# The S5 loop of a four-branch decoder layer in another order, with its outputs put in order by transfers

## The chip, the cores and the metric

The kernel runs on one core of a Trainium2 chip. The metric is the device time of one execution, in microseconds (us); less is better. A core has five engines that work side by side and wait for one another by semaphores: TensorE (PE in the profile; its weight loads are PEld), VectorE (DVE), ScalarE (ACT), GpSimd (POOL) and SyncE (SP), which here issues all transfers. Each engine takes its instructions strictly in the order of the program.

## The reference, cut to what matters

A layer runs four branches on one projected input and merges them. The change lies in branch B, a diagonal complex state-space model (S5) of 64 channel groups of 16 channels, each with one complex state of 64 dimensions:

```python
def _s5(u, state0_re, state0_im, a_re, a_im, log_dt, b_re, b_im, c_re, c_im, d_skip):
    ...
    lam_bar = jnp.exp(lam * dt)
    b_bar = ((lam_bar - 1.0) / lam)[..., None] * lax.complex(b_re.astype(f32), b_im.astype(f32))
    ug = u.reshape(bsz, t, S5_GROUPS, S5_GROUP)
    bu = jnp.einsum('gnc,btgc->btgn', b_bar, ug.astype(jnp.complex64))
    h0 = lax.complex(state0_re.astype(f32), state0_im.astype(f32))
    bu = bu.at[:, 0].add(lam_bar * h0)
    ...
    h = jax.vmap(lambda bseq: lax.associative_scan(combine, (a_el, bseq))[1])(bu)
    y = jnp.einsum('gcn,btgn->btgc', c, h).real.reshape(bsz, t, BR_WIDTH) + d_skip * u
    return y, h[:, -1].real, h[:, -1].imag
...
    y_b = jax.nn.gelu(y_b)
    y_b = y_b * jax.nn.sigmoid(jnp.matmul(y_b, s5_glu_w.astype(f32)) + s5_glu_b) * jax.nn.silu(z_s5)
```

Branch D, an attention into 256 memory tokens whose values `cache_mem_v` are read for eight samples, is touched in one place.

## The kernel before, in words

The 512 prompt tokens and the 32 tokens of eight samples lie side by side as 544 columns; the 1024 channels lie in eight tiles of 128 partitions. A large product is made in *units*: `unit` (L166) loads a tile of 1024 x 128 weights (`raw`, three buffers), ScalarE casts its high part to `whi` (L177), VectorE takes the rest to `wlo` (L64, called from L178), and TensorE makes 48 matmuls `pu` of 272 columns (L188). `whi`, `wlo` and `pu` have two buffers each.

The S5 stage runs over eight tiles f of eight groups. The prompt is cut into 64 blocks of 8 steps. `s5_in` (L708) projects `u`, reorders it on ScalarE and VectorE into `uf`, and brings it by two transfers (`ud`, `U`) to rows of step and channel. `s5_mats` (L725) builds the block matrices: powers of the transition times B (`bm`), transposed by TensorE (`pbt`) and copied to `bt`; powers times C (`cm`), where each difference of `q1` and `q2` is written by four operations of 64 partitions, since real and imaginary parts go to the lower and upper half; and from `cm` and `bbs` the Toeplitz blocks (`pk`, `kt`), spread by transfers through `kd` into `tp`. `s5_scan` (L784) makes the block inputs (`pvr`, `pvi`), turns and scans them on VectorE and GpSimd (`gr`, `gi`, `t1` to `t4`), writes the states to the halves of `hs`, their last column to `hp`, and the samples' states to `hn`, which read `pvr` and `pvi` last. `s5_y` (L838) makes `py` from `U`, `tp`, `cm` and `hs`, copies it to `yj` and takes it through DRAM (`yd`) to `yt`, with one transfer each way. There the partitions stand in the order channel, group; `s5_out` (L856) multiplies by the permutation `permid` on TensorE, which orders them as group, channel and the columns as time (`pn`), and applies GELU by ScalarE and VectorE into `stag`. `s5_rot` (L650) makes the turning factors of two tiles on GpSimd, some 36 small operations.

Between these pieces stand units of the generator `gd` (L697: gates and down projection of branch D), so that TensorE has work while the others run. The loop (L874 to L887) is, for each f: `s5_scan(f)`, `s5_mats(f+1)`, `s5_out(f-1)`, a unit, `s5_y(f)`, `s5_in(f+2)`, in most turns a second unit, and behind f = 0, 2, 4 `s5_rot`. Behind the loop come the GLU and the scan of branch A. A scheduler may move instructions past one another; what each engine runs in the end is shown below for the places that matter. Accumulators of a bank each (`bk`) come from a ring of four, shared by `pbt`, `pk`, `pvr`, `pvi`, `py` and `pn`; `bm`, `q1`, `q2`, `hs`, `yj` and `uf` have one buffer (`yj` and `uf` share one), `U` has two.

Of the kernel before, what the change touches and what calls it, by code (L numbers as in the profile page):

```python
# [34 lines left out]
def hybrid_kernel(ctx: ExitStack, tc: tile.TileContext, I, O):  # L35
# [9 lines left out]
    def ctile(shape, name, dt=F32):  # L45
        return cst.tile(shape, dt, name=name, tag=name)
# [56 lines left out]
    permid = ctile([P, P], "permid")  # L103
    V.tensor_copy(permid.rearrange("p (g c) -> p g c", c=16), ident.rearrange("p (c g) -> p g c", g=8))
# [560 lines left out]
    for b in range(NB):  # L665
        step(hd)
        step(su, 2)
        pm = xv.tile([P, 8, TS], F32, name="pmx", tag="qmx")
        tt(G, pm, pts.rearrange("p m (h t) -> p (m h) t", h=4), bc(bmask[:, b, :], 1, 8), MUL)
        for m in range(2):  # L670
            vb = xv.tile([P, D], F32, name="vb", tag="vb")
            dma(vb, I["cache_mem_v"][0, b, m * P:(m + 1) * P].rearrange("p h d -> p (h d)"))
            for h in range(4):
                T.matmul(pacc[32 * h:32 * h + 32, 0:256], pm[:, 4 * m + h, :], vb[:, h * 256:(h + 1) * 256],
                         start=b == 0 and m == 0, stop=b == 7 and m == 1, tile_position=(0, 32 * h))
# [32 lines left out]
    def s5_in(f):  # L708
        pu = unit(wcols(C_U + f * P), x2, perm=True)
        uf = s5r.tile([P, 8, NV], F32, name="uf", tag="uf", bufs=1)  # L710
        G.memset(uf[:, 4:8, 0:8], 0.0)
        G.memset(uf[:, 0:4, 72:80], 0.0)
        S.copy(uf[:, :, 8:42], pu[:, 0, 0:272].rearrange("p (k s) -> p s k", s=8))
        S.copy(uf[:, :, 42:72], pu[:, 1, 0:240].rearrange("p (k s) -> p s k", s=8))
        us = pu[:, 1, 240:272].rearrange("p (b t) -> p t b", t=4)
        V.tensor_copy(uf[:, 0:4, 0:8], us)
        V.tensor_copy(uf[:, 4:8, 72:80], us)  # L717
        U = s5r.tile([P, 8, NV], F32, name="U", tag="U", bufs=2)
        ud = s5d.tile([8, P, NV], F32, name="ud", tag="ud")
        dma(ud.rearrange("q p k -> p q k")[:, ::-1], uf)  # L720
        dma(U, ud.rearrange("q (c g) k -> (q c) g k", g=8))

        return U

    def s5_mats(f):  # L725
# [9 lines left out]
        bt = s5r.tile([P, 2, 4, P], F32, name="bt", tag="bt")  # L735
        for ri in range(2):
            pb = bank("pbt")
            for a in range(4):
                T.transpose(pb[:, a * P:(a + 1) * P], bm[:, ri, a].rearrange("p l c -> p (l c)"), ident)
            copy(S if ri else V, bt[:, ri].rearrange("p a n -> p (a n)"), pb)  # L740
# [7 lines left out]
        tt(V, q2, e4(pwi, 9), ctif, MUL)  # L748
        for g2 in range(2):
            pr = slice(64 * g2, 64 * g2 + 64)  # L750
            tt(V, cmv[0:64, :, g2], q1[pr], q2[pr], SUB)
# [3 lines left out]
        tt(G, q2, e4(pwr, 9), ctif, MUL)  # L755
        for g2 in range(2):
            pr = slice(64 * g2, 64 * g2 + 64)
            stt(cmv[64:128, :, g2], q1[pr], -1.0, q2[pr], MUL, SUB)

        bbs = s5r.tile([P, 4, 2, 16], F32, name="bbs", tag="bbs", bufs=2)  # L760
        for ri, src in enumerate((bbr, bbi)):
            for g2 in range(2):
                dma(bbs[64 * ri:64 * ri + 64, :, g2, :], src[64 * g2:64 * g2 + 64, gs])

# [19 lines left out]
    def s5_scan(f, U, bt, E):  # L784
# [35 lines left out]
        tt(G, t4, E[:, 1], gr, MUL)  # L820
        for g2 in range(2):
            pr = slice(64 * g2, 64 * g2 + 64)
            tt(V, hsv[0:64, :, g2, 9:73], t1[pr], t2[pr], SUB)
            tt(V, hsv[64:128, :, g2, 9:73], t3[pr], t4[pr], ADD)
            for ri in range(2):
                S.copy(hsv[64 * ri:64 * ri + 64, :, g2, 0:8], h0[pr, ri, :, gs].rearrange("p b a -> p a b"))
# [11 lines left out]
    def s5_y(f, U, cm, tp, hs_):  # L838
# [14 lines left out]
        dma(yt, yd.rearrange("(j c) g k -> (c g) j k", c=16))  # L853
        return yt

    def s5_out(f, yt):  # L856

        pn = [bank("pn0"), bank("pn1")]
        T.matmul(pn[0][:, 0:272], permid, yt[:, :, 8:42].rearrange("p j k -> p k j"), start=True, stop=True)
        T.matmul(pn[1][:, 0:240], permid, yt[:, :, 42:72].rearrange("p j k -> p k j"), start=True, stop=True)  # L860
        T.matmul(pn[1][:, 240:272], permid, yt[:, 0:4, 0:8].rearrange("p j b -> p b j"), start=True, stop=True)
        for a in range(2):
            y = pn[a][:, 0:HALF]
            ga = stag[f][:, a * HALF:(a + 1) * HALF]
            S.activation(ga, y, AF.Square, scale=GSQ)
            stt(ga, ga, 0.7978845608028654, y, ADD, MUL)
            S.activation(ga, ga, AF.Tanh)
            stt(ga, ga, 1.0, y, ADD, MUL)

    us_, mt_, yt = [s5_in(0)], s5_mats(0), None  # L870
# [3 lines left out]
    for f in range(8):  # L874
        bt, cm, tp, E = mt_
        hs_ = s5_scan(f, us_[f], bt, E)
        if f < 7:
            mt_ = s5_mats(f + 1)
# [3 lines left out]
        yt = s5_y(f, us_[f], cm, tp, hs_)  # L882
        if f < 6:
            us_.append(s5_in(f + 2))
        step(gd, (0, 1, 1, 1, 1, 0, 1, 1)[f])
        if f % 2 == 0 and f // 2 + 1 in range(1, 4):
            s5_rot(f // 2 + 1)  # L887
# [863 lines left out]
```

## Time and profile before

| | |
|---|---|
| median of three runs | 1483.68 us (1482.52 to 1487.28) |
| the profiled execution | 1485.23 us, of which its span is 1483.3 |
| TensorE busy | 1417.8 us, 96% of the span |
| VectorE, ScalarE, GpSimd busy | 60%, 33%, 23% |
| moved by the transfers | 172.96 MB, mean 117 GB/s |

The profile is that of one execution. A row of a group names the line, the engine, the operation, what it writes and reads, and how often; behind it come the busy time, the mean of one in ns, and how long its engine sat idle ahead of it and for whom. A row of waits says who waited for whom: sum in us, number, longest. A row of the timeline begins with start and duration; matmuls overlap, so the distance between starts is their pace.

### The profile page before, as it was taken

Reading aid. Unit: us, or ns where it says so; the run is one execution under the profiler, and the core shown is the slowest. Engines: PE = TensorE matmul, PEld = TensorE weight load, DVE = VectorE, ACT = ScalarE, POOL = GpSimd, SP = SyncE. Lnnn points to the kernel's source line nnn. Section 1 sums busy time; section 2 is a strip of 40 time slices with the busy share of each in tenths; the row PEclk is TensorE's granted clock in tenths of the full one; section 3 lists DMA queues with packets and bytes.
Section 4 is the critical chain, followed back from the end, with each engine's and each line's share of the span. In section 5 each row is a group of like instructions: output and inputs, shape, how many; then the busy total and the mean of one; then the engine's idle time right before and its main releaser. Section 6 shows DMA issues by size and latency. Waiting matters only on the chain. (4 is left out here: it accounts for less than half of the span.)

```text
span 1483.3 us, 28633 instructions
## 1 busy us (share of the span) xinstructions
PE 1417.8 (96%) x11761; PEld 1346.1 (91%) x11761; DVE 887.9 (60%) x1739; ACT 491.0 (33%) x849; POOL 338.3 (23%) x511
## 2 busy tenths in 40 slices
PE   6999998889889999999999999999999999899997
PEld 6998888778778999999999899999999998789997
DVE  5355497887877594677777544544343455454553
ACT  4244234223223432433333331333232332114232
POOL 2010233757672111002222222000000011110222
PEclk9999999999999999999999999899999999999999
DMA  8577362546536323322222464132323235663341
GB/s 204 165 214 235 105 199 65 122 95 150 121 96 131 88 80 90 86 72 78 73 77 74 115 181 135 46 89 60 93 62 89 68 111 172 200 198 115 99 147 61
DMA packets 298500, 172.96 MB, mean 117 GB/s; under 512 B 46365, under 2 KB 289385, under 8 KB 298370
## 3 DMA queue, kind: packets, MB, share of 16 engines
q1 hardware_dynamic: 298370, 171.14, 41.9%
q8 instruction: 92, 1.51, 0.4%
q14 instruction: 38, 0.31, 0.1%
HBM read 145.35 MB, written 25.24 MB: 115 GB/s over the span
## 5 line engine op out<-in xcount | busy, mean ns | idle before, releaser
L188 PE MATMUL pu<-xh,whi 128*128 128x272 f32 (+1 forms) x2000 | 430.6, 294 | 0.7 <-DVE uf L717 0.5
L188 PE MATMUL pu<-xl,whi 128*128 128x272 f32 (+1 forms) x2000 | 430.9, 293 | 0.1
L188 PE MATMUL pu<-xh,wlo 128*128 128x272 f32 (+1 forms) x2000 | 427.9, 292 | 0.0
L64 DVE TENSOR_TENSOR wlo<-raw,whi 128x1024 fp32r<-128x1024 f32 x181 | 249.4, 1378 | 220.0 <-ACT whi L177 215.9
L177 ACT CAST whi<-raw 128x1024 fp32r<-128x1024 f32 x181 | 198.6, 1097 | 485.0 <-PE pu L188 368.5
L188 PEld LDWEIGHTS pu<-xh,whi 128*128 128x128 f32 x2000 | 321.4, 191 | 6.6 <-issue 5.3
L188 PEld LDWEIGHTS pu<-xl,whi 128*128 128x128 f32 x2000 | 322.2, 191 | 5.5 <-issue 4.5
L188 PEld LDWEIGHTS pu<-xh,wlo 128*128 128x128 f32 x2000 | 319.8, 191 | 3.8 <-issue 3.3
L188 PE MATMUL pu<-oh,wlo 128*128 128x272 f32 x640 | 134.6, 290 | 2.3 <-DVE wlo L64 2.3
L188 PE MATMUL pu<-ol,whi 128*128 128x272 f32 x640 | 136.4, 291 | 0.0
L188 PE MATMUL pu<-oh,whi 128*128 128x272 f32 x640 | 136.1, 292 | 0.0
L188 PEld LDWEIGHTS pu<-oh,wlo 128*128 128x128 f32 x640 | 101.5, 190 | 3.2 <-DVE wlo L64 2.6
L188 PEld LDWEIGHTS pu<-ol,whi 128*128 128x128 f32 x640 | 102.3, 190 | 1.9 <-issue 1.7
L188 PEld LDWEIGHTS pu<-oh,whi 128*128 128x128 f32 x640 | 101.8, 189 | 1.8 <-issue 1.5
L64 POOL TENSOR_TENSOR merged<-merged,gt 128x544 f32<-128x544 f32 x18 | 28.1, 1564 | 139.8 <-DVE gt L67 139.7
L67 DVE SCALAR_TENSOR_TENSOR cb<-cb,dcm,pcn 128x257 f32<-128x257 f32 x64 | 28.7, 478 | 25.6 <-PE pcn L1584 25.3
L67 DVE SCALAR_TENSOR_TENSOR cc<-cc,dcm,pcu 128x257 f32<-128x257 f32 x24 | 11.5, 478 | 44.6 <-PE pcu L1463 44.6
L188 PE MATMUL pu<-mh,whi 128*128 128x256 f32 x128 | 37.8, 295 | 0.1
L64 POOL TENSOR_TENSOR SS<-SS,dec 128x128 f32<-128x128 f32 x24 | 19.5, 814 | 77.6 <-DVE SS L1223 49.8
L188 PE MATMUL pu<-mlo,whi 128*128 128x256 f32 x128 | 37.1, 290 | 0.0
L188 PE MATMUL pu<-mh,wlo 128*128 128x256 f32 x128 | 36.2, 283 | 0.0
L1446 POOL MEMSET vtl<- 128x2 f32 x16 | 1.6, 99 | 143.3 <-PE pcu L1463 140.3
(638 smaller groups left out, 2238.3 us busy)
## 6 DMA issues: line engine op xcount, KB each, us to landing
raw<-in_w_in_dram SPq DMA_DIRECT2D x124, 512.0 KB
raw<-in_w_down_dram SPq DMA_DIRECT2D x32, 512.0 KB
kb<-in_cache_mem_k_dram SPq DMA_DIRECT2D x8, 1024.0 KB
raw<-in_w_mem_kv_dram SPq DMA_DIRECT2D x16, 512.0 KB
vb<-in_cache_mem_v_dram SPq DMA_DIRECT2D x16, 512.0 KB
cb<-in_state_mlstm_c_dram SPq DMA_DIRECT2D x16, 512.0 KB
out_dram<-cb SPq DMA_DIRECT2D x16, 512.0 KB
tp<-kd SPq DMA_DIRECT2D x16, 256.0 KB
```

What stands on the lines that cost most here:

```text
L64: eng.tensor_tensor(out, a, b, op)
L67: V.scalar_tensor_tensor(out, a, s, b, op0, op1)
L177: S.copy(hv, rv)
L188: T.matmul(ps[:, a, 0:c1 - c0], wt[:, k, :], xt[:, k, c0:c1], start=first, stop=last)
L1446: G.memset(vtl[:, 256:258].bitcast(F32), 0.0)
```

## The change

In each turn of the loop `s5_y(f)` now stands last, behind `s5_in(f+2)`, the second part of the matrices (`s5_mats2(f+1)`: transposition, Toeplitz blocks and their transfers, split from `s5_mats`) and both units. `U` gets a third buffer. `permid` and `pn` are gone: eight transfers bring `yd` to `yt` with the partitions in the order group, channel, and GELU works on `yt` with step ahead of block; a copy on ScalarE puts its result into the order of time. The differences for `cm` and the sums for `hs` are made on all 128 partitions, and ScalarE copies the halves to their places. The copy of the first half of `bt` and two small copies to `uf` go from VectorE to ScalarE. In branch D the two tiles of cached values of a sample are loaded ahead of both products.

```diff
@@ -100,8 +100,6 @@
     ident = ctile([P, P], "ident")
     make_identity(nc, ident)
-    permid = ctile([P, P], "permid")
-    V.tensor_copy(permid.rearrange("p (g c) -> p g c", c=16), ident.rearrange("p (c g) -> p g c", g=8))
     ones = ctile([P, P], "ones")
     G.memset(ones, 1.0)
     ecol = ctile([P, 1], "ecol")
@@ -667,11 +665,14 @@
         step(su, 2)
         pm = xv.tile([P, 8, TS], F32, name="pmx", tag="qmx")
         tt(G, pm, pts.rearrange("p m (h t) -> p (m h) t", h=4), bc(bmask[:, b, :], 1, 8), MUL)
+        vbs = []
         for m in range(2):
             vb = xv.tile([P, D], F32, name="vb", tag="vb")
             dma(vb, I["cache_mem_v"][0, b, m * P:(m + 1) * P].rearrange("p h d -> p (h d)"))
+            vbs.append(vb)
+        for m in range(2):
             for h in range(4):
-                T.matmul(pacc[32 * h:32 * h + 32, 0:256], pm[:, 4 * m + h, :], vb[:, h * 256:(h + 1) * 256],
+                T.matmul(pacc[32 * h:32 * h + 32, 0:256], pm[:, 4 * m + h, :], vbs[m][:, h * 256:(h + 1) * 256],
                          start=b == 0 and m == 0, stop=b == 7 and m == 1, tile_position=(0, 32 * h))
     step(hd, 16)
     step(su, 4)
@@ -713,9 +714,9 @@
         S.copy(uf[:, :, 8:42], pu[:, 0, 0:272].rearrange("p (k s) -> p s k", s=8))
         S.copy(uf[:, :, 42:72], pu[:, 1, 0:240].rearrange("p (k s) -> p s k", s=8))
         us = pu[:, 1, 240:272].rearrange("p (b t) -> p t b", t=4)
-        V.tensor_copy(uf[:, 0:4, 0:8], us)
-        V.tensor_copy(uf[:, 4:8, 72:80], us)
-        U = s5r.tile([P, 8, NV], F32, name="U", tag="U", bufs=2)
+        S.copy(uf[:, 0:4, 0:8], us)
+        S.copy(uf[:, 4:8, 72:80], us)
+        U = s5r.tile([P, 8, NV], F32, name="U", tag="U", bufs=3)
         ud = s5d.tile([8, P, NV], F32, name="ud", tag="ud")
         dma(ud.rearrange("q p k -> p q k")[:, ::-1], uf)
         dma(U, ud.rearrange("q (c g) k -> (q c) g k", g=8))
@@ -732,12 +733,6 @@
         q2 = s5r.tile([P, 4, 9, 16], F32, name="q2", tag="sc2")
         bbrf, bbif = bc(bbr[:, gs, :], 2, 8), bc(bbi[:, gs, :], 2, 8)
         cmul(V, G, bm[:, 0], bm[:, 1], e4(pwr, 8), e4(pwi, 8), bbrf, bbif, q1[:, :, 0:8, :], q2[:, :, 0:8, :])
-        bt = s5r.tile([P, 2, 4, P], F32, name="bt", tag="bt")
-        for ri in range(2):
-            pb = bank("pbt")
-            for a in range(4):
-                T.transpose(pb[:, a * P:(a + 1) * P], bm[:, ri, a].rearrange("p l c -> p (l c)"), ident)
-            copy(S if ri else V, bt[:, ri].rearrange("p a n -> p (a n)"), pb)
         cm = s5r.tile([P, 8, 9, 16], F32, name="cm", tag="cm", bufs=2)
         cmv = cm.rearrange("p (a b) l c -> p a b l c", b=2)
@@ -746,21 +741,30 @@
         q2 = s5r.tile([P, 4, 9, 16], F32, name="q2", tag="sc2")
         tt(G, q1, e4(pwr, 9), ctrf, MUL)
         tt(V, q2, e4(pwi, 9), ctif, MUL)
+        tt(V, q1, q1, q2, SUB)
         for g2 in range(2):
-            pr = slice(64 * g2, 64 * g2 + 64)
-            tt(V, cmv[0:64, :, g2], q1[pr], q2[pr], SUB)
+            S.copy(cmv[0:64, :, g2], q1[64 * g2:64 * g2 + 64])
         q1 = s5r.tile([P, 4, 9, 16], F32, name="q1", tag="sc1")
         q2 = s5r.tile([P, 4, 9, 16], F32, name="q2", tag="sc2")
         tt(G, q1, e4(pwi, 9), ctrf, MUL)
         tt(G, q2, e4(pwr, 9), ctif, MUL)
+        stt(q1, q1, -1.0, q2, MUL, SUB)
         for g2 in range(2):
-            pr = slice(64 * g2, 64 * g2 + 64)
-            stt(cmv[64:128, :, g2], q1[pr], -1.0, q2[pr], MUL, SUB)
+            S.copy(cmv[64:128, :, g2], q1[64 * g2:64 * g2 + 64])
         bbs = s5r.tile([P, 4, 2, 16], F32, name="bbs", tag="bbs", bufs=2)
         for ri, src in enumerate((bbr, bbi)):
             for g2 in range(2):
                 dma(bbs[64 * ri:64 * ri + 64, :, g2, :], src[64 * g2:64 * g2 + 64, gs])
+        return bm, cm, bbs
+    def s5_mats2(f, bm, cm, bbs):
+        bt = s5r.tile([P, 2, 4, P], F32, name="bt", tag="bt")
+        for ri in range(2):
+            pb = bank("pbt")
+            for a in range(4):
+                T.transpose(pb[:, a * P:(a + 1) * P], bm[:, ri, a].rearrange("p l c -> p (l c)"), ident)
+            S.copy(bt[:, ri].rearrange("p a n -> p (a n)"), pb)
         pk = bank("pk")
         for g2 in range(2):
@@ -818,10 +822,12 @@
         tt(G, t2, E[:, 1], gi, MUL)
         tt(V, t3, E[:, 0], gi, MUL)
         tt(G, t4, E[:, 1], gr, MUL)
+        tt(V, t1, t1, t2, SUB)
+        tt(V, t3, t3, t4, ADD)
         for g2 in range(2):
             pr = slice(64 * g2, 64 * g2 + 64)
-            tt(V, hsv[0:64, :, g2, 9:73], t1[pr], t2[pr], SUB)
-            tt(V, hsv[64:128, :, g2, 9:73], t3[pr], t4[pr], ADD)
+            S.copy(hsv[0:64, :, g2, 9:73], t1[pr])
+            S.copy(hsv[64:128, :, g2, 9:73], t3[pr])
             for ri in range(2):
                 S.copy(hsv[64 * ri:64 * ri + 64, :, g2, 0:8], h0[pr, ri, :, gs].rearrange("p b a -> p a b"))
         V.tensor_copy(hp[:, 8 * f:8 * f + 8], hs_[:, :, 72])
@@ -850,24 +856,27 @@
         yt = s5r.tile([P, 8, 72], F32, name="yt", tag="yt")
         yd = s5d.tile([P, 8, 72], F32, name="yd", tag="yd")
         dma(yd, yj)
-        dma(yt, yd.rearrange("(j c) g k -> (c g) j k", c=16))
+        for j in range(8):
+            dma(yt[:, j, :], bass.AP(tensor=yd.tensor, offset=yd.offset + j * 16 * 576, ap=[[72, 8], [576, 16], [1, 72]]))
         return yt
     def s5_out(f, yt):
-        pn = [bank("pn0"), bank("pn1")]
-        T.matmul(pn[0][:, 0:272], permid, yt[:, :, 8:42].rearrange("p j k -> p k j"), start=True, stop=True)
-        T.matmul(pn[1][:, 0:240], permid, yt[:, :, 42:72].rearrange("p j k -> p k j"), start=True, stop=True)
-        T.matmul(pn[1][:, 240:272], permid, yt[:, 0:4, 0:8].rearrange("p j b -> p b j"), start=True, stop=True)
-        for a in range(2):
-            y = pn[a][:, 0:HALF]
-            ga = stag[f][:, a * HALF:(a + 1) * HALF]
-            S.activation(ga, y, AF.Square, scale=GSQ)
-            stt(ga, ga, 0.7978845608028654, y, ADD, MUL)
-            S.activation(ga, ga, AF.Tanh)
-            stt(ga, ga, 1.0, y, ADD, MUL)
-
-    us_, mt_, yt = [s5_in(0)], s5_mats(0), None
+        ga = stag[f]
+        parts = ((yt[:, :, 8:72], ga[:, 0:TP].rearrange("p (j k) -> p j k", j=8), ga[:, 0:TP].rearrange("p (k j) -> p j k", j=8)),
+                 (yt[:, 0:4, 0:8], ga[:, TP:NT].rearrange("p (t b) -> p t b", t=4), ga[:, TP:NT].rearrange("p (b t) -> p t b", t=4)))
+        for y, t, _ in parts:
+            S.activation(t, y, AF.Square, scale=GSQ)
+            stt(t, t, 0.7978845608028654, y, ADD, MUL)
+        S.activation(ga, ga, AF.Tanh)
+        for y, t, _ in parts:
+            stt(y, t, 1.0, y, ADD, MUL)
+        for y, _, o in parts:
+            S.copy(o, y)
+    us_, yt = [s5_in(0)], None
+    mt_ = s5_mats2(0, *s5_mats(0))
     step(gd)
     us_.append(s5_in(1))
     step(gd)
@@ -875,14 +884,16 @@
         bt, cm, tp, E = mt_
         hs_ = s5_scan(f, us_[f], bt, E)
         if f < 7:
-            mt_ = s5_mats(f + 1)
+            ma = s5_mats(f + 1)
         if f > 0:
             s5_out(f - 1, yt)
         step(gd)
-        yt = s5_y(f, us_[f], cm, tp, hs_)
         if f < 6:
             us_.append(s5_in(f + 2))
+        if f < 7:
+            mt_ = s5_mats2(f + 1, *ma)
         step(gd, (0, 1, 1, 1, 1, 0, 1, 1)[f])
+        yt = s5_y(f, us_[f], cm, tp, hs_)
         if f % 2 == 0 and f // 2 + 1 in range(1, 4):
             s5_rot(f // 2 + 1)
     s5_out(7, yt)
```

How this moves instructions is shown at three places, each in one turn of the loop. On TensorE, before, the product of `yt` with `permid` stands in the middle of a unit (`pu`), some way behind `pk`:

```order
L859 MATMUL pn_4088<-yt,permid 128x272
L188 MATMUL pu<-xl,whi 128x272
L188 MATMUL pu<-xh,wlo 128x272 x2
L188 MATMUL pu<-xh,whi 128x272 x2
L188 MATMUL pu<-xl,whi 128x272 x2
L860 MATMUL pn_4089<-yt,permid 128x240
L861 MATMUL pn_4089<-yt,permid 128x32
```

With the change these rows are gone; two whole units follow `pvr` and `pvi`, then `pbt` and `pk` stand together, and the next unit behind them:

```order
L186 MATMUL pu<-xl,whi 128x272 x2
L186 MATMUL pu<-xh,wlo 128x272 x2
L766 MATMUL pbt<-ident,bm 128x128 x8
L772 MATMUL pk<-cm,bbs 32x128 x8
L186 MATMUL pu<-oh,whi 128x272 x2
L186 MATMUL pu<-ol,whi 128x272 x2
```

So `pbt` and `pk` moved from near the turn's start to behind its first two units. On ScalarE, before, `yj` is followed by the states' first columns, a cast and the next input:

```order
L849 COPY yj<-py 128x288 x2
L826 COPY hs<-h_1836 64x4x8 x4
L177 CAST whi<-raw 128x1024
L713 COPY uf<-pu 128x8x34
L714 COPY uf<-pu 128x8x30
L177 CAST whi<-raw 128x8x8x16
L59 COPY bt<-pbt 128x512
L772 COPY kt<-pk 128x256
```

With the change the copies of the halves of `cm` (`q` are its products) and of `hs` (`t` are the sums) follow, and the first operation of GELU on `yt` stands among them:

```order
L855 COPY yj<-py 128x288 x2
L832 COPY hs<-h_1834 64x4x8 x4
L746 COPY cm<-q_4838 64x4x144 x2
L753 COPY cm<-q_4845 64x4x144 x2
L830 COPY hs<-t_4801 64x4x64 x2
L870 ACTIVATE st_2888<-yt 128x32
L175 CAST whi<-raw 128x1024
L829 COPY hs<-t_4799 64x4x64 x2
```

What moved is that two of the four copies to `hs` now stand behind an operation that needs `yt`. On SyncE, before, one transfer each takes `yj` out and brings `yt` in:

```order
L780 DMA tp<-kd_2949 128x4x128 x2
L82 DMA raw<-in_w_down_dram 128x8x128
L852 DMA yd<-yj 128x576
L853 DMA yt<-yd 128x8x72
L82 DMA raw<-in_w_in_dram 128x8x128
L720 DMA ud<-uf 128x8x80
```

With the change:

```order
L82 DMA raw<-in_w_in_dram 128x8x128
L784 DMA tp<-kd_2947 128x4x128 x2
L82 DMA raw<-in_w_in_dram 128x8x128
L858 DMA yd<-yj 128x576
L861 DMA yt<-yd 128x1x72 x8
L82 DMA raw<-in_w_down_dram 128x8x128
L758 DMA bbs<-bbr 64x4x16 x2
L721 DMA ud<-uf 128x8x80
```

Eight transfers stand where one stood, and a weight load, `bbs` and the next `ud` stand behind them.

## The prediction

> **What bounds the kernel now.** The first view is the page's head: busy time of each engine over the span.
>
> ```profile
> PE 1417.8 (96%) x11761; PEld 1346.1 (91%) x11761; DVE 887.9 (60%) x1739; ACT 491.0 (33%) x849; POOL 338.3 (23%) x511
> ```
>
> TensorE is the bound, and all other engines matter only where they make it wait. So I looked for the stage in which TensorE loses most, first by a window of the S5 stage, from the first `pbt` to the last `phq` (length, TensorE busy, granted clock, share of the DMA engines, GB/s), then by who is waited for in it (sum, times, longest).
>
> ```profile
> 260.58:505.40 244.82, 215.05 (x2139) 0.94 0.50 116
> PE pn L859 <- DVE bt L61: 6.4, 3, 4.5
> PE pk L768 <- DVE cm L67: 4.5, 3, 2.4
> PE py L848 <- DVE hs L64: 3.7, 1, 3.7
> PE pk L768 <- ACT bt L59: 3.1, 1, 3.1
> PE pbt L739 <- POOL bm L64: 2.5, 1, 2.5
> PE pu L188 <- DVE wlo L64: 2.3, 1, 2.3
> PE py L848 <- DVE hn L64: 1.8, 2, 1.0
> ```
>
> These waits, with 4.9 us of others (one of them for `yt`, quoted below), are 29.2 us; and the granted clock is 0.94 of full speed. The timeline gives the pace of each TensorE group when nothing is in its way (start, duration; the pace is the distance of starts).
>
> ```profile
> 353.81 0.41 PE L188 MATMUL pu<-xh,whi 128*128 128x272 f32 x2
> 354.06 0.41 PE L188 MATMUL pu<-xl,whi 128*128 128x272 f32 x2
> ...
> 355.02 0.35 PE L848 MATMUL py<-U,tp 128*64 128x72 f32 x4
> ...
> 357.17 0.39 PE L188 MATMUL pu<-xl,whi 128*128 128x272 f32 x1
> ...
> 276.24 0.35 PE L791 MATMUL pvr<-U,bt 128*64 128x72 f32 x4
> ...
> 277.44 1.09 PE L739 MATMUL pbt<-ident,bm 128*128 128x128 f32 x8
> 278.29 0.50 PE L188 MATMUL pu<-oh,whi 128*128 128x272 f32 x2
> ...
> 370.62 0.97 PE L768 MATMUL pk<-cm,bbs 128*32 128x128 f32 x16
> 371.52 0.39 PE L188 MATMUL pu<-xh,whi 128*128 128x272 f32 x1
> ...
> 499.92 1.14 PE L859 MATMUL pn<-yt,permid 128*128 128x272 f32 x2
> 500.88 1.04 PE L860 MATMUL pn<-yt,permid 128*128 128x240 f32 x2
> 501.74 0.33 PE L861 MATMUL pn<-yt,permid 128*128 128x32 f32 x2
> 501.90 0.28 PE L891 MATMUL pho<-ident,hp 128*64 128x128 f32 x1
> ```
>
> A unit matmul comes every 0.125 us, so a unit (48) is 6.0 us; `py` takes 2.15, `pv` 1.20, `pbt` 0.85, `pk` 0.90, and `pn` 0.96 + 0.86 + 0.16 = 1.98. The program has 1123 unit matmuls in this stretch and each small group eight times: 140.4 + 17.2 + 9.6 + 6.8 + 7.2 + 15.8 + 0.5 for the closing transposes = 197.5 us. The stretch lasts 244.8, so **47.3 us are lost**: 29.2 waiting, 18.1 at the low clock and in small gaps. What a wait leaves behind is seen here:
>
> ```profile
> 343.21 0.64 PE L768 MATMUL pk<-cm,bbs 128*32 128x128 f32 x16 [3.14 <-ACT bt L59]
> ...
> 344.78 0.66 PE L188 MATMUL pu<-xh,whi 128*128 128x272 f32 x2
> 345.24 0.66 PE L188 MATMUL pu<-xl,whi 128*128 128x272 f32 x2
> ```
>
> After an idle stretch of 3.14 us pairs come every 0.46 instead of 0.25, for some 3.4 us: 1.6 us more. The 2.3 us behind `wlo` had the same effect; waits of 1.8 had none. I charge 1.6 to each wait above 2 us. The Trainium skill, "TensorE: Matmul & The Clock Gate", section "Part 1: The HAM clock gate", puts the fall to half rate after an idle window of about 3.4 us; this trace shows it after shorter waits. By the page the waits forecast below 3.4 us would cost only themselves, and the sum would be some 6 us lower; the row decides.
>
> **The change, part by part.**
>
> *`pn` goes* (8 x 1.98): **15.8 us** off TensorE's own work, with no work in its place there.
>
> *The waits in front of `pn`* (6.4 + 2.1 us) go with it. The other waits depend on the new order: after `py` TensorE goes straight to the next `pv`, two units, `pbt`, `pk`, a unit, `py`. Between `py`'s end and `pk` stand 1.20 + 12.0 + 0.85 = **14.05 us** of work; all other engines have that long. `pk` takes the accumulator bank that `pvr` had, and that is free only when VectorE has done its last read in `hn`. Ahead of that read on VectorE stands the copy to `hp`, which needs ScalarE's copies into `hs`; and among these, in ScalarE's new order, stands the `Square` that waits for `yt`. So two chains meet at `pk`.
>
> *The chain through `yt`.* These rows price it: a copy to `yj`, SyncE's waits for `yd`, its issue of `yt` and TensorE's wait for it, and two issues of `tp`.
>
> ```profile
> L849 ACT COPY yj<-py 128x288 f32<-128x288 f32 x16 | 6.2, 397 | 19.7 <-PE py L848 18.2 <-issue 1.5
> SPq L853 <- DMA yd<-yj: 37.1, 8, 7.1
> 477.49 0.36 SPq L853 DMA_DIRECT2D yt<-yd  x1
> 480.88 1.29 PE L859 MATMUL pn<-yt,permid 128*128 128x272 f32 x2 [2.10 <-DMA yt<-yd]
> 383.82 1.28 SPq L780 DMA_DIRECT2D tp<-kd  x2
> ```
>
> The copy 0.5 with its hand-over, `yd`'s issue 0.35, its landing 37.1 / 8 = 4.6, eight issues instead of one, the last landing 480.88 - 477.85 = 3.0. No row shows a small `yt` issue: 0.36 by its own row, 0.64 by `tp`'s; I take 0.5, nearer to the larger form, 4.0 in all. That is 12.5 us. Behind it follow the small `Square`, two to four copies to `hs`, a gate's `Tanh`, `hp`, `hn` and one GELU step: about 4 us, so `pk` at 16.5 to 17, **3 us late**. The bounds: landing in 2 us and the cheap issue give 8.8 and no wait; landing in 7.1 and 0.64 give 16.1 and 6.5 us. While SyncE waits for `yd` and issues eight times, the next weight loads and `bbs`, `ud` stand behind it. A weight tile is loaded about one period (23 us) before its cast, which covers that; uncovered, it would be 4 us a period.
>
> *The chain through the scan*: `yj`, the four copies of `h0`, now two copies to `cm` before POOL may reuse `q1`, `q1`, `gr`, the eight scans, `t1` to `t4`, `hs`.
>
> ```profile
> L826 ACT COPY hs<-h 64x32 f32<-64x32 f32 x32 | 7.9, 248 | 0.3
> L59 ACT COPY kbt<-pkt 128x512 f32<-128x512 f32 x16 | 9.4, 586 | 20.9 <-PE pkt L447 20.8
> L64 POOL TENSOR_TENSOR q<-pwi,ctr 128x576 f32<-128x576 f32 x8 | 10.9, 1358 | 16.9 <-DVE cm L64 16.9
> L64 POOL TENSOR_TENSOR gr<-gr,t 128x256 f32<-128x256 f32 x8 | 6.8, 850 | 2.1 <-DVE t L64 2.1
> L807 DVE TENSOR_TENSOR_SCAN gr<-rho,gr 128x64 f32<-128x64 f32 x32 | 12.6, 453 | 3.5 <-POOL gr L64 3.5
> 305.00:334.60 29.60, 24.90 (x216) 22.35 (x216) 27.19 (x47) 7.31 (x18) 14.03 (x16) 0.88 0.31 76
> 334.60:364.50 29.90, 26.76 (x271) 25.06 (x270) 21.27 (x43) 10.28 (x21) 23.13 (x49) 0.94 0.69 157
> ```
>
> 0.5 + 4 x 0.25 + 2 x 0.6 + 1.4 + 0.85 + 8 x 0.45, then by the same rows about 1.5 for POOL's last product, 0.5 for the difference, 4 x 0.4 for `hs` and 0.8 to the end of `hn` make 13 us: in time. But in every second period POOL also has the rotation: 23.1 us busy against 14.0 (columns: TensorE, its loads, VectorE, ScalarE, POOL), which is a whole new period of 23.1 (three units and 5.1). It runs over by about 4 us, so `pk` waits about 4 us in the period behind each of the three rotations, instead of the 3 above, not on top.
>
> *The moves to ScalarE*: on VectorE, `cm` falls from four operations on 64 partitions to two on 128, `hs` from four to two.
>
> ```profile
> L64 DVE TENSOR_TENSOR cm<-q,q 64x576 f32<-64x576 f32 x16 | 12.0, 750 | 6.6 <-POOL q L64 3.7 <-PE py L848 2.8
> L64 DVE TENSOR_TENSOR hs<-t,t 64x256 f32<-64x256 f32 x32 | 14.9, 467 | 1.0
> ```
>
> The pass over 64 partitions takes as long as one over 128, so this saves 2 x 0.75 + 2 x 0.47 = 2.4; with half of `bt` and the small copies of `uf` (an estimate from ScalarE's 0.59 for 128x512 and 0.25 for 64x32: 1) some 3.5 us a period leave VectorE. ScalarE takes 4 copies to `cm`, 4 to `hs`, `bt`, `uf` and the two reorderings in the output, 6 us by the same rows. VectorE was busy 21 to 27 of 30 us, ScalarE 7 to 10; both fit into 26. The copies' place in the chains is counted above; elsewhere I cost them at nothing, since units run beside them. Without that cover it is the 6 us a period.
>
> *The rest*: the pairs of `vb` leave the order of instructions as it was, and `permid`'s copy falls into the start, where VectorE waits for `x`: nothing, at most 1 us either way.
>
> **Sum.** Waits: 1.8 at the first `pk` as now, 4 + 3 + 4 + 3 + 4 in periods 1 to 5 (period 0 has no `yt`), 3 in period 6, which has a unit less in front, 1 in period 7, and 1 before the GLU, whose input now comes through `yt` and six steps while three units run: 25 us. Seven of them above 2 us: 11 for the clock. So 36 are lost instead of 47.3. The profiled execution, 1485.2 us (its span and 1.9 around it), loses 15.8 + 11.3 = 27 and comes to 1458. The median shown, 1483.7, is 1.5 lower, so the forecast is **1456**.
>
> **Rivals.** *The transfers arrive in time.* For it: `yd` landed within about 2 us where few loads were queued; against: in the new order a weight load and two `tp` are issued just ahead of it. Only the rotations' waits stay: 15 us idle, 6 for the clock, so 15.8 + 26 off: **1442**.
>
> *The transfers are dearer* (the upper bounds, 5 us a period rather than 3): 10 to 14 more, **1469**.
>
> *VectorE or POOL becomes the bound*, in order and stretched by each other. For it: 27.2 of 29.6 us in one window; against: 3.5 less work. At periods near 30 us nothing is gained: **1483**.
>
> *Slower: `yt` in series.* If each small transfer ends before the next begins, 8 x (0.36 + 3.0) = 27 us follow `yd`, `pk` waits some 18 us in six periods, 108 + 20 are lost, and the time is about **1550**. It decides from a mean wait near 8 us a period (63 us lost). Against: two issues of `tp` follow one another in 0.64 us without waiting. The Trainium skill speaks for this rival in "DMA: Bandwidth & Descriptors": about 2.0 us fixed for each transfer ("Anatomy of one DMA"), and transfers under 64 KB dominated by descriptors ("Measured"); these are 36 KB. By eight such fixed costs in a row the sum would be about 1495; no row of this trace shows small transfers in series.
>
> **How the numbers follow.** Forecast (1447 to 1468) 0.47; in time (1427 to 1447) 0.24; dearer (1468 to 1479) 0.15; no change 0.07; slower 0.07. 0.3% is 4.4 us, about what a measurement can tell: faster 0.86, same 0.07, slower 0.07. The range 1428 to 1478 leaves out 0.16.
>
> **What would show it.** No `pn` on TensorE; `pk <- DVE hn` as its longest wait in the stage, some 3 us each; ScalarE's `Square` waiting for `yt`; SyncE showing eight `yt` issues of about 0.5; POOL without pause in periods 0, 2, 4. Wrong it would be if `pk` or `py` waited for `cm` or `hs` instead, if units waited for `wlo` or weights, or if the GLU waited long for `oh`.

## The result, and the profile after

| | before | changed |
|---|---|---|
| median beside each other on one chip | 1484.13 us (1480.98 to 1490.07) | 1477.06 us (1472.15 to 1485.15), 15 runs each |
| ratio | | 0.9949, 95% interval 0.9938 to 0.9960 |
| the profiled execution's span | 1483.3 us | 1476.0 us |

The change brings some 7 us; the forecast said 28. The page's head of the changed kernel, and a window of its S5 stage from the first `pbt` to the last `phq` (length, TensorE, its loads, VectorE, ScalarE, GpSimd, then granted clock, share of the DMA engines, GB/s):

```profile
PE 1397.2 (95%) x11713; PEld 1335.3 (90%) x11713; DVE 865.3 (59%) x1682; ACT 535.8 (36%) x945; POOL 335.7 (23%) x511
```

```profile
261.65:491.20 229.55, 186.22 (x2024) 178.64 (x2023) 161.87 (x301) 115.60 (x230) 135.09 (x211) 0.91 0.50 116
```

TensorE is 20.6 us less busy, but the span is only 7.3 shorter. The stage shows why. By the paces of the prediction its work is now 1055 unit matmuls (68 of the former 1123 have slid behind it) and the small groups without `pn`, 173.2 us; it lasts 229.55, so 56.3 us are lost where 47.3 were. Of these TensorE waits 43.3; the view of its waits (sum, times, longest) in that window:

```profile
PE pk L772 <- ACT st L870: 7.7, 1, 7.7
PE pk L772 <- DVE s L64: 7.3, 1, 7.3
PE pk L772 <- ACT cm L753: 6.2, 3, 5.5
PE pu L186 <- ACT gt L215: 5.8, 3, 3.3
PE phq L909 <- ACT yj L855: 4.1, 1, 4.1
PE phq L909 <- DVE hn L64: 3.2, 1, 3.2
PE pk L772 <- DVE hn L64: 2.6, 1, 2.6
PE py L854 <- ACT hs L830: 2.4, 1, 2.4
...
```

So 15.8 us of work went and 9.0 of losses came: 6.8 net. `pk` waits as foreseen, but longer; units wait for a gate's `Tanh` (`gt`), and the two closing transpositions wait 7.3 us, which was not foreseen. The waits by turn of the loop, from the timeline:

| turn | start | 0 | 1 | 2 | 3 | 4 | 5 | 6 | 7 | end |
|---|---|---|---|---|---|---|---|---|---|---|
| forecast, us | 1.8 | 0 | 4 | 3 | 4 | 3 | 4 | 3 | 1 | 1 |
| measured, us | 0.7 | 2.5 | 8.8 | 3.3 | 7.7 | 3.3 | 7.3 | 2.4 | 0 | 7.3 |

Turns 2, 4 and 6 came near their forecast in size. The odd ones, each behind a rotation, and the end did not. Turn 3 of the changed kernel shows what is late. First TensorE and SyncE (start, duration):

```profile
359.03 0.34 PE L795 MATMUL pvr<-U,bt 128*64 128x72 f32 x4
...
381.19 1.08 PE L772 MATMUL pk<-cm,bbs 128*32 128x128 f32 x16 [7.70 <-ACT st L870]
```

```profile
360.92 1.28 SPq L784 DMA_DIRECT2D tp<-kd  x2
362.24 4.95 SPq L82 DMA_DIRECT2D raw<-in_w_in_dram  x2
367.23 1.14 SPq L858 DMA_DIRECT2D yd<-yj  x1
372.50 4.89 SPq L861 DMA_DIRECT2D yt<-yd  x8
```

`yj` was copied by 359.64, but SyncE comes to `yd` 7.6 us later, behind `tp` and two weight loads that wait for their buffers. Then VectorE in the same turn:

```profile
359.47 1.59 DVE L64 TENSOR_TENSOR q<-pwi,bbr 128x512 f32<-128x512 f32 x1 [3.58 <-POOL st L64]
360.98 0.68 DVE L64 TENSOR_TENSOR bm<-bm,q 128x512 f32<-128x512 f32 x1
361.58 0.71 DVE L67 SCALAR_TENSOR_TENSOR merged<-gt,pu 128x544 f32<-128x544 f32 x1
362.85 1.77 DVE L64 TENSOR_TENSOR q<-pwi,cti 128x576 f32<-128x576 f32 x1 [0.56 <-POOL bm L64]
364.54 2.23 DVE L64 TENSOR_TENSOR wlo<-raw,whi 128x1024 fp32r<-128x1024 f32 x1
366.66 0.75 DVE L64 TENSOR_TENSOR q<-q,q 128x576 f32<-128x576 f32 x1
367.33 0.41 DVE L64 TENSOR_TENSOR gr<-st,pvr 128x256 f32<-128x256 f32 x1
```

`pv` is done at 360.2, but the scan's first read of it (`gr`) is at 367.33: VectorE has the next tile's matrices ahead of it, and their first step had to wait for the rotation, which uses the same scratch. The view of the waits names a different instruction for `pk` in each of turns 2 to 5 (`whi`, `st`, `hn`, `s`). By the timeline `pk` starts in all four 0.2 to 0.3 us behind the end of VectorE's last read of `pvi` (`hn`), which frees a bank: in turn 3 that read ends at 380.98 and `pk` starts at 381.19. So what counts in these turns is what holds up VectorE ahead of `hn`. From the start of `pv` to `pk`, in the columns of the window above, it is nearly full in turn 3 and not in turn 2:

```profile
330.01:345.79 15.78, 14.30 (x143) 14.02 (x139) 9.63 (x22) 6.00 (x13) 7.55 (x17) 1.00 0.55 134
359.03:381.19 22.16, 14.46 (x143) 14.09 (x140) 19.57 (x32) 8.25 (x18) 14.36 (x16) 0.92 0.51 113
```

So two suspects stand behind the 43.3 us, transfers and VectorE with GpSimd, and a third, the bank that `pk` takes over.

### The profile page after: what moved, and what is told of

It is laid out like the page before. It is cut to its first block, busy times and chain, and to the rows that moved or that the text cites. A ratio compares the mean times of both kernels' runs of the same rounds, so it can differ in the third digit from the quotient of the medians.

```text
span 1476.0 us, 28630 instructions
## 1 busy us (share of the span) xinstructions
PE 1397.2 (95%) x11713; PEld 1335.3 (90%) x11713; DVE 865.3 (59%) x1682; ACT 535.8 (36%) x945; POOL 335.7 (23%) x511
## 5 line engine op out<-in xcount | busy, mean ns | idle before, releaser
L186 PE MATMUL pu<-xl,whi 128*128 128x272 f32 (+1 forms) x2000 | 425.6, 291 | 0.1
L67 DVE SCALAR_TENSOR_TENSOR cb<-cb,dcm,pcn 128x257 f32<-128x257 f32 x64 | 28.6, 478 | 25.9 <-PE pcn L1595 25.6
```

Of the source, the lines that this page charges most:

```text
L67: V.scalar_tensor_tensor(out, a, s, b, op0, op1)
L186: T.matmul(ps[:, a, 0:c1 - c0], wt[:, k, :], xt[:, k, c0:c1], start=first, stop=last)
```

## The experiments

Eighteen kernels, all edits of the changed kernel but for `old_order_yt`. All ratios are to the kernel before, timed beside it on one chip; the last column is (ratio - 1) x 1484 us. The changed kernel itself stands at -7.6.

| kernel | edit | ratio (95% interval) | us |
|---|---|---|---|
| one_yt | one transfer for `yt` | 1.0026 (1.0013 to 1.0040) | +3.9 |
| rot_first | rotations ahead of the loop | 0.9980 (0.9967 to 0.9993) | -3.0 |
| rot_own | own scratch for the rotation | 0.9929 (0.9915 to 0.9944) | -10.5 |
| hn_early | `hn` ahead of the scan | 0.9955 (0.9943 to 0.9968) | -6.7 |
| yj_yt | `yj` in `yt`'s buffer | 0.9952 (0.9935 to 0.9969) | -7.1 |
| yj_rot | yj_yt + rot_own | 0.9964 (0.9950 to 0.9978) | -5.3 |
| yj_hn | yj_yt + hn_early | 0.9934 (0.9914 to 0.9953) | -9.8 |
| no_yt | no transfers `yd`, `yt` | 0.9861 (0.9845 to 0.9877) | -20.6 |
| noyt_split | no_yt, rotation in two parts | 0.9865 (0.9843 to 0.9886) | -20.0 |
| yd_act | ScalarE issues `yd` | 0.9886 (0.9869 to 0.9902) | -16.9 |
| one_act | yd_act + one_yt | 1.0015 (1.0000 to 1.0030) | +2.2 |
| act_split | yd_act, rotation in two parts | 0.9879 (0.9858 to 0.9900) | -18.0 |
| act_split_hn | act_split + yj_hn | 0.9865 (0.9844 to 0.9887) | -20.0 |
| old_order_yt | before + transfers for `pn` only | 0.9963 (0.9950 to 0.9976) | -5.5 |
| old_all | all but the loop's order | 0.9939 (0.9920 to 0.9958) | -9.1 |
| old_all_act | old_all + yd_act | 0.9930 (0.9908 to 0.9952) | -10.4 |
| new_order_pn | `pn` put back | 1.0048 (1.0029 to 1.0067) | +7.1 |
| halves_dve | halves by VectorE | 1.0002 (0.9991 to 1.0013) | +0.3 |

### The suspects one by one

```diff
 one_yt
-        dma(yd, yj)
-        for j in range(8):
-            dma(yt[:, j, :], bass.AP(tensor=yd.tensor, offset=yd.offset + j * 16 * 576, ap=[[72, 8], [576, 16], [1, 72]]))
+        dma(yd.rearrange("(c j) g k -> j c (g k)", j=8), yj)
+        dma(yt, bass.AP(tensor=yd.tensor, offset=yd.offset, ap=[[72, 8], [8 * 576, 16], [576, 8], [1, 72]]))
 rot_first
-    for q in range(1):
+    for q in range(4):
         s5_rot(q)
 rot_own
-                ts_ = [... for t in ("sc1", "sc2")]
+                ts_ = [... for t in ("sc1", "rt2")]
```

In *hn_early* the block that computes `hn` (from `p4` on) moves from the end of `s5_scan` to ahead of the scans, with scratch of its own.

> Changed kernel, but yd is written with the channel ahead of the half-tile, so that one transfer instead of eight brings yt. Theory Y (ScalarE stands in its order at Square, waiting for yt, with the copies of hs, a gate's Tanh and yj behind it): SyncE's issue of yt falls from 4.9 us to about 0.6, TensorE's waits in the periods without a rotation (3.3 and 3.3), the one for hs (2.4) and the closing one for yj (4.1) go, 10 to 15 us in all: 1461 to 1468. Theory R (what counts are the three waits of 5.5 to 7.7 us of pk in the periods behind a rotation on GpSimd): those stay, 1469 to 1474. Theory B (what counts is the bank that pk takes over from pvr, freed late in VectorE's order): 1472 to 1477.

> Changed kernel, but all four rotations are made ahead of the S5 loop (scratch in merged), none in it. Theory R: the waits of pk in periods 1, 3 and 5 (5.5, 7.7, 7.3 us) fall to about 2 each and 4 us of low clock go with them, 15 to 19 us: 1458 to 1463, unless GpSimd then holds up the start of the loop, which would show as waits of pbt or of the first units. Theory Y: Square's wait holds hs and hn in these periods too, the waits stay above 4: 1470 to 1477. Theory B alone: the bank comes free some 7 us earlier too, since its first readers no longer stand behind GpSimd; it expects as theory R here.

> Changed kernel, but the rotation has one scratch tile of its own where it shared that of VectorE's product q for the next tile. Theory R in its narrow form (VectorE waits for GpSimd because of the shared scratch, 6.7, 3.6 and 3.6 us, with the scan's first reads of pvr behind): these waits go and pk waits 3 us less in each of the three periods: 1463 to 1468. Theory R in its wide form (GpSimd's own time for the rotation delays its products of the next tile and of the scan): the wait moves to VectorE's next step, 1473 to 1478. Theory Y: 1473 to 1477.

> Changed kernel, but hn, the last reader of pvr and pvi, is computed ahead of the scan instead of behind hs (scratch of its own). Theory B: pk no longer waits for VectorE's hn and s or behind ScalarE's Square (7.7 + 7.3 + 2.6 + 1.5 us), py not for hn (1.6), the first phq not for hn (3.2): some 20 us of waiting and 5 of low clock, of which hs may give a part back at py: 1452 to 1462. Theories R and Y: the same chains now end at py by way of hs, and cm and the gate's Tanh are as late as they were: 1466 to 1475.

*one_yt* is slower than the changed kernel by some 11 us, which no theory had. ScalarE's wait for `yt`, of the changed kernel and then of one_yt, in 285 to 485 us:

```profile
ACT st L870 <- DMA yt<-yd: 18.2, 7, 5.5
```

```profile
ACT st L869 <- DMA yt<-yd: 23.6, 4, 7.8
```

The issue fell to 0.6 us as expected, but the first `Square` needs the whole transfer and starts 4.1 to 6.5 us behind the end of that issue. With eight, in the two turns where the large `Square` stood waiting for the last of them, it started 1.8 and 1.9 us behind the end of the last issue. The edit also writes `yd` in another order, so this run does not separate that from the single transfer.

*rot_first* takes the rotations out, yet `pk` now waits in turns 2 to 5 alike (4.1 to 5.8 us each), and the start pays: the first `pbt` is at 269.00 instead of 261.65. GpSimd's and TensorE's waits in it:

```profile
POOL uf L712 <- DMA yd<-yj: 21.5, 4, 6.3
```

```profile
PE pk L772 <- ACT hs L829: 23.4, 4, 6.9
```

From the first `pv` to the last the loop took 187.1 us, where the changed kernel took 190.6. So without a rotation another chain is nearly as long. *rot_own* stands 3 us better, hardly clear of the intervals and less than the narrow form expected: VectorE's 13.8 us of waiting for the rotation's `st` became 16.5 us of waiting for GpSimd's `bm`. *hn_early* empties the waits of `pk` for VectorE, and the time does not move, since units now wait for the `Tanh` that ScalarE has behind `hs`:

```profile
PE pu L186 <- ACT gt L215: 18.5, 4, 5.5
```

So the bank alone is not the cause; it is where the lateness showed.

### GpSimd's wait for the shared buffer

`yj` and `uf` share a buffer; GpSimd stands at the memset of `uf` until `yd` has been read from it, 13.3 us in the changed kernel, with the scan's products behind.

```diff
-        yj = s5r.tile([P, 8, 72], F32, name="yj", tag="uf")
+        yj = s5r.tile([P, 8, 72], F32, name="yj", tag="yt")
```

> Changed kernel, but yj takes the buffer of yt and no longer that of uf. Theory P (GpSimd stands in its order at the memset of uf until yd has been read out of the shared buffer, 13.3 us in four waits, and the products t of the scan stand behind it, so hs and all that ScalarE has behind hs come late): these waits are gone, VectorE's waits for t (5.2 and 4.7 us) go, and pk and the units of periods 2 and 4 wait 1 instead of 3.3 us each; periods 1, 3 and 5 keep the rotation: 1467 to 1473. Theories R and Y: nothing of weight changes, 1474 to 1479.

> The edit of yj_yt together with that of rot_own. If GpSimd has two independent hold-ups, the shared scratch of the rotation and the shared buffer of yj, the gains add: rot_own gave 3 us against the changed kernel, yj_yt should give 4 to 8, together 1464 to 1471. If the rotation's own time is the limit in periods 1, 3 and 5, it is no better than the better one of the two, 1468 to 1474.

> The edit of yj_yt together with that of hn_early. In hn_early the waits of pk were gone, but units waited 18.5 us for the gate's Tanh, which stands on ScalarE behind hs and Square. Theory P: hs comes 5 us earlier in periods 2 and 4, and the waits for the Tanh fall from 18.5 to some 9 us: 1462 to 1469. Theory Y: the Tanh still stands behind Square, waiting for yt: 1472 to 1477.

Against the changed kernel none of the three moves by more than the intervals, and *yj_rot* loses again what rot_own had gained. In *yj_yt* GpSimd's wait is gone, but what it hid comes out, ScalarE's wait for `yt`:

```profile
ACT st L870 <- DMA yt<-yd: 33.8, 9, 6.9
```

Two chains of about the same length end at the same place; shortening one shows the other.

### The transfers themselves

```diff
 no_yt
-        dma(yd, yj)
-        for j in range(8):
-            dma(yt[:, j, :], ...)
-        return yt
+        return yj
 yd_act
-        dma(yd, yj)
+        S.dma_start(yd, yj)
```

> Changed kernel with the transfers yd and yt left out: yj takes the buffer of yt and GELU reads yj itself, so the rows of branch B stand in another order than the reference's. Nothing else is removed. Theory Y2 (a cycle closes each turn: py, yj, yd's issue behind other transfers on SyncE, its landing, yt's eight issues and landing, Square on ScalarE with hs behind it, then pk or py; about 30 us a turn where TensorE has 23 us of work): without the transfers the turns fall to 24 to 25 us, TensorE's waits in the stage from 43 to under 15 us, 1440 to 1455. Theory S (the scan's chain on VectorE and GpSimd alone is as long as the cover): the waits of 4 to 7 us a turn stay, 1468 to 1478.

> Changed kernel, but yd is issued by ScalarE directly behind the copy to yj, where SyncE has it some 4 us later, behind tp and a weight load. Theory Y2: yt comes 3 to 5 us earlier in each of seven turns, less 0.5 to 1 us of ScalarE's time for the issue; 2 to 3 us of each turn's wait go: 1455 to 1466. Theory S: no gain, or a loss by ScalarE's issue: 1474 to 1482.

> yd_act with one transfer for yt in place of eight. If the single transfer is worse in itself (in one_yt the first Square waited for the whole of it, 4.2 to 6.5 us behind the issue, where with eight the small Square starts when four have landed): 6 to 11 us above yd_act, 1472 to 1478. If it was worse only because yd came late: within 3 us of yd_act, 1463 to 1469.

*no_yt* bounds all that `yd` and `yt` cost: 13 us. *yd_act* gets 9.3 of these back with one word. TensorE's waits in the stage fall from 43.3 us to 34.3 in yd_act and 30.5 in no_yt, so most of them remain without any of these transfers. In its turn 3, `pv` starts at 353.95:

```profile
353.85 0.73 ACT L855 COPY yj<-py 128x288 f32<-128x288 f32 x2
354.46 1.03 ACT L832 COPY hs<-h 64x32 f32<-64x32 f32 x4
356.07 0.33 ACTq L858 DMA_DIRECT2D yd<-yj  x1
```

```profile
357.85 4.89 SPq L82 DMA_DIRECT2D raw<-in_w_in_dram  x2
362.79 6.11 SPq L861 DMA_DIRECT2D yt<-yd  x8
```

`yd` leaves 2.1 us behind `pv`'s start instead of 8.2, while the same two loads are issued; `yt` begins at 8.8 instead of 13.5. It beats both kernels, and nothing below beats it by more than the intervals. *one_act* shows that the single transfer, with the order of `yd` that it needs, is the worse one also where `yd` leaves early, 19 us above yd_act; in part because its issue also stands later in SyncE's order (in turn 4 at 400.33, where yd_act has 393.01). Why one such transfer lands later than the last of eight was not tried.

### What is left in the odd turns

The rotation is cut: five doublings in the even turn, the sixth in the odd one.

```diff
-        if f % 2 == 0 and f // 2 + 1 in range(1, 4):
-            s5_rot(f // 2 + 1)
+        if f < 6:
+            s5_rot(f // 2 + 1, range(5, 6) if f % 2 else range(5))
```

> yd_act with each rotation cut into two parts: five doublings in the even turn, the sixth (6 us of GpSimd's 15) in the odd one. Theory R (GpSimd's time, since VectorE stands at the shared scratch with the scan's first reads behind): the waits of pk behind the rotations (5.5, 6.5 us and the clock) fall by 2 to 4 us each: 1454 to 1462. If these waits are set by yt or hs: within 3 us of yd_act, 1463 to 1469.

> act_split with the edits of yj_yt and hn_early. If the hold-ups add (bank of pvr, memset of uf, rotation, late yd): another 3 to 8 us below act_split, 1448 to 1458. If one of them was already covered by the others: as act_split.

> no_yt with each rotation cut in two, as in act_split; GELU reads yj, so the rows of branch B are not in the reference's order. If the two waits of 8.7 us left in no_yt are the rotation's: 8 to 14 us below no_yt, 1448 to 1454. If they are VectorE's and GpSimd's work of two turns, run in order and stretched by each other (a product bm takes 1.6 us where 0.7 alone): 1458 to 1463, with VectorE busy over 80% of an odd turn.

None of them gains over yd_act or no_yt by more than the interval. So cutting the rotation this way does not free the odd turns; it also moves a part of GpSimd's work into them, so it does not show what a turn free of it would take. Turns 2 and 3 together take 61.5 us in the changed kernel, 55.8 in yd_act, 56.7 in act_split, and 58.3 and 58.0 in no_yt and noyt_split. Nor need the long turns be those behind a rotation: in one_act turns 2 and 4 take 35.4 and 35.3 us, turns 3 and 5 24.4 and 25.6. Turns 2 and 3 of *act_split*, and turn 3 of *noyt_split* from `pv` to `pk`, in the columns of the window above:

```profile
332.16:355.47 23.31, 23.14 (x271) 22.48 (x268) 18.75 (x33) 14.76 (x31) 19.52 (x41) 1.00 0.60 140
355.47:388.87 33.40, 26.07 (x271) 25.03 (x268) 28.20 (x45) 15.00 (x32) 20.81 (x20) 0.85 0.54 123
```

```profile
356.02:380.00 23.98, 14.58 (x143) 14.08 (x141) 22.58 (x37) 12.03 (x28) 17.88 (x18) 0.88 0.39 86
```

Turn 2 now runs at TensorE's own 23.1 us, with no wait above 0.2 us. But VectorE gets only 18.75 us done in it and 28.20 in the next: what it left over is ahead of the next scan. Over both turns it is busy 46.95 of 56.71 us, so it is held by its order in the long turn rather than by the sum of its work. In noyt_split, with no transfer and the rotation split, VectorE is busy 22.58 of the 23.98 us from `pv` to `pk`, and `pk` waits 8.8 of them:

```profile
355.80 1.77 DVE L64 TENSOR_TENSOR bm<-pwr,bbr 128x512 f32<-128x512 f32 x1
...
361.63 2.82 DVE L64 TENSOR_TENSOR wlo<-raw,whi 128x1024 fp32r<-128x1024 f32 x1
364.33 0.20 DVE L67 SCALAR_TENSOR_TENSOR st<-st,yj 128x32 f32<-128x32 f32 x1
364.43 0.43 DVE L64 TENSOR_TENSOR gr<-st,pvr 128x256 f32<-128x256 f32 x1
...
380.06 1.23 DVE L64 TENSOR_TENSOR wlo<-raw,whi 128x1024 fp32r<-128x1024 f32 x1
381.20 0.68 DVE L64 TENSOR_TENSOR bm<-pwr,bbr 128x512 f32<-128x512 f32 x1
```

From `pv` to `pk` the bound is VectorE there, in order and stretched: the same product takes 1.77 us beside GpSimd and 0.68 alone. Over the whole of turn 3 it is busy 27.52 of 34.90 us, 79%, just under what was expected. That VectorE's order holds the long turns is read from the traces and not shown by a run: no kernel was run that gives VectorE less to do in these turns, nor one with neither transfers nor rotations in the loop. The one run that gives it more, halves_dve below, is slower, though it also takes copies off ScalarE.

### The parts of the change

`old_order_yt` is the kernel before with `s5_y`, `s5_out` and `permid` as changed; `old_all` has this loop:

```diff
 old_all
-            ma = s5_mats(f + 1)
+            mt_ = s5_mats2(f + 1, *s5_mats(f + 1))
         ... s5_out(f - 1, yt); step(gd)
+        yt = s5_y(f, us_[f], cm, tp, hs_)
         ... s5_in(f + 2); step(gd, ...)
-            mt_ = s5_mats2(f + 1, *ma)
-        yt = s5_y(f, us_[f], cm, tp, hs_)
 halves_dve: cm by tt and stt, hs by tt, in halves as in the kernel before
 new_order_pn: s5_out, permid and the one transfer for yt as in the kernel before
```

> The kernel before with one part of the change alone: pn and permid are gone, eight transfers bring yt, GELU works on yt; the order of the loop, cm, hs, bt, uf and vb are as before. If the new order is what made the new waits: the 15.8 us of pn and some of its 8.5 us of waits come off, 1462 to 1469, better than the whole change. If taking pn away exposes the same chains in any order (a turn is then one pn shorter for all other engines): 1472 to 1480. If the old order hides the transfers worse, since py stands ahead of the next products: above 1484.

> Changed kernel, but with yt brought by one transfer as in the kernel before, and ordered by permid and pn on TensorE again (15.8 us of work). If the waits of the new order are set by the chain through yd and yt, TensorE now stands at pn itself or its waits shrink by what pn covers: 1476 to 1488, pn costing less than its 15.8. If pn and the waits add: 1489 to 1496.

> Changed kernel, but the differences for cm and the sums for hs are written by VectorE in halves of 64 partitions as before (2.4 us more on VectorE a turn), and ScalarE's eight copies are gone (4.5 us a turn). Prediction on record (the moves cost and bring nothing, units lie beside them): 1475 to 1479. Theory A (ScalarE's order is what delays hs: Square and a gate's Tanh stand among its copies): hs no longer waits there, 1464 to 1471. Theory V (VectorE is the tighter engine): 1480 to 1488.

> The whole change except the order of the loop: the turn is scan, both parts of the matrices, out, a unit, y, in, a unit, as in the kernel before. Theory O (the new order is worth nothing or costs: with halves on VectorE the changed order stood at 1482.4 against 1478.2 for the old order): the placing by ScalarE adds its 8 us to the old order with transfers, 1466 to 1472. Theory N (the new order is what makes the placing by ScalarE worth something, since it gives it cover): 1476 to 1482.

> old_all with yd issued by ScalarE. If the late issue of yd belongs to the new order alone (there tp and a weight load are issued between yj and yd): as old_all, within 4 us. If it is the same in the old order: 6 to 10 us below old_all.

In the new order putting `pn` back, with its single transfer and its way of GELU, costs 14.7 us (+7.1 against -7.6), near the 15.8 of `pn`'s own work; TensorE then stands in front of it for `yt`:

```profile
PE pn L867 <- DMA yt<-yd: 28.4, 6, 7.5
```

In the old order, putting the transfers in place of `pn` alone brings 5.5. The placing by ScalarE is worth 7.9 us in the new order (+0.3 against -7.6); in the old one, with the small moves, 3.6, which the intervals hardly part from nothing. And the order by itself brings nothing: all without it stands at -9.1, all with it at -7.6, with overlapping intervals. The late `yd` belongs to the new order: issuing it from ScalarE gains 9.3 us there and 1.3, within the interval, in the old one. With `yd` issued by ScalarE in both, the new order is ahead by 6.5 us (-16.9 against -10.4), clear of the intervals: the order is worth something only once `yd` leaves early.

## Why the prediction was wrong, point by point

- **`pn` goes, 15.8 us**: right; no `pn` is left on TensorE, and putting it back costs 14.7, though with one transfer for eight in the same edit.
- **The clock, 1.6 us for each wait over 2 us**: near in the sum, in part by luck. Eight such waits make 12.8; lost beside the waits are 56.3 - 43.3 = 13.0. (The forecast's 11 counts seven such waits, but its own list has six, 9.6.) Wait by wait the charge does not hold: the 2.4 of turn 6 leaves no slow pace behind it, while turn 2, whose waits are 1.5 and 1.8, runs at 0.45 us a pair from 348.2 to 353.8; and in the kernel before seven such waits make 11.2 where 18.1 were lost. The page's window of about 3.4 us (the Trainium skill, "TensorE: Matmul & The Clock Gate", "Part 1: The HAM clock gate") would count four of them, 6.4; the trace goes with the shorter waits.
- **The sum of the waits, "25 us"**: wrong, and this is the step that failed; 43.3 measured. The 12 us of the three turns behind a rotation were 23.8, the closing 1 was 7.3. Two of its terms were mis-sized, the head of the chain through `yt` and the scan's chain behind a rotation; the next points take them in turn. Turns 2 and 4 came at 3.3 for 3, but in part by another path. The prediction had `hn` wait for `hp` and the copies to `hs`; in turns 2 to 5 the read of `pvi` that frees the bank stands ahead of `hp`. In turns 2 and 4 GpSimd's products of the scan stand behind its memset of `uf`, which waits 6.2 and 5.7 us for `yd` in the shared buffer, a wait that the prediction does not have; in turn 4 the GELU step on VectorE, behind `Square`, holds `hn` as well.
- **The chain through `yt`, 12.5 us and then 4 more**: mis-sized at its head. The sum counted `yd`'s issue from its own duration, with nothing ahead of it. The prediction did note what stands *behind* these issues on SyncE, and, among the rivals, that a load and two `tp` stand ahead, but gave that no price. `yd` was issued 4.2 to 8.2 us behind the start of `pv`, and this alone is worth 9.3 us by yd_act. The transfers also make the end: ScalarE stands at `Square` for `yt` of tile 6, 5.5 us, and `yj` of tile 7, which frees the bank of the second `phq`, stands behind. Without the transfers 0.3 us is left of the 7.3; with `yd` early 4.7 are. The rest of the chain was near: eight issues in 4.9 us for 4.0, the last landing some 1.9 us behind for 3.0.
- **GpSimd "runs over by about 4 us" behind each rotation**: too small (5.5 to 7.7 at `pk`), not worked out from a row, and of the wrong kind. The sum let the scan's chain begin as soon as `pv` was there, each operation at its mean time. VectorE's order has the next tile's matrices ahead of the scan's first read, which comes 8.3 us behind the start of `pv` in turn 3. Cutting the rotation in two did not help.
- **The moves to ScalarE, costed "at nothing" since "both fit into 26"**: wrong on the good side by 7.9 us. What fits, though no run parts VectorE's share from ScalarE's, is that VectorE is nearly full from `pv` to `pk` in every second turn, which the mean over a turn hid, so that each product taken off it counts there.
- **The rival "VectorE or POOL becomes the bound"**, given 0.07, names what seems to hold the odd turns, and turns 1 to 5 did last 28 to 33 us. It was set against by the busy time of whole windows, where the stretch from `pv` to `pk` should have been looked at.
- **The rival "`yt` in series"**: did not come. The eight are issued 0.6 us apart and overlap; the fixed cost in the Trainium skill's "DMA: Bandwidth & Descriptors", section "Anatomy of one DMA", which that page gives for transfers issued by GpSimd, is not paid eight times in a row here, where SyncE issues them. (The rival's sum was low by its own terms: with the 4 us behind `yt` that the forecast's chain has, `pk` would wait 22 us a turn and not 18.)
- **The signs named beforehand**: `Square` waiting for `yt` and eight issues of some 0.6 us were seen; `pk` for `hn` appears only once under that name, but by the timeline in turns 2 to 5. GpSimd was not without pause in turns 2 and 4: it stood 6.2 and 5.7 us for `yd`. Of the signs against, `pk` for `cm` (5.5 us in turn 1) and `py` for `hs` (2.4 us in turn 6) were there too.

## What to carry to other kernels

Price a transfer from the moment its data is ready, with everything that stands ahead of its issue in the queue's order, not from the issue; if that is the longest part, another engine's queue may be free. Where one engine's lateness shows at a bank, a buffer and an activation in turn, as each is removed, look for what all of them wait on before mending the one that the profile names. A mean busy share of 70% over two turns may be one full turn and one easy one: look at the stretch between the two instructions that matter.

## What the runs showed of the hardware that was not expected

What waited for one transfer of 288 KB in rows of 288 B went on 4.1 to 6.5 us after the end of its issue; behind the last of eight transfers with the same rows it was 1.8 and 1.9 us. One product of VectorE took 1.77 us where GpSimd worked beside it and 0.68 where it did not (`bm`, above), 2.6 times as long. And stretches that are alike in both kernels may differ by some us in one execution: of the 7.3 us between the two spans, 4.4 are there when `spX` starts, just behind the stage (514.86 and 510.45); most of the rest comes between 800 and 950 us, where among others the kernel before ran 50 us at a granted clock of 0.90 and the changed one the same stretch at 1.00 (in the 50 us ahead of it the changed one had 0.97 and the kernel before 1.00); why was not tried:

```profile
900.00:950.00 50.00, 50.00 (x387) 46.93 (x386) 17.46 (x28) 12.14 (x21) 9.30 (x11) 0.90 0.33 90
```

```profile
895.60:945.60 50.00, 50.00 (x421) 47.22 (x421) 20.84 (x32) 14.05 (x24) 9.37 (x12) 1.00 0.33 90
```
